# A hybrid decoder layer: how its first transfers, its warm-up and one row of scalings are laid out

## The chip, the cores and the metric

The kernel runs on one core of a Trainium2 chip. The time is device microseconds of the core, the median of several runs: 1089.81 us before, with runs from 1089.6 to 1090.01. The engines are TensorE (PE; its weight loads are shown as PEld), VectorE (DVE), ScalarE (ACT), GpSimd (POOL) and SyncE (SP). Transfers are issued on the queues of SP (q1 in the profile), ScalarE (q10) and GpSimd (q0).

## The reference, cut to what matters

One layer of 256 tokens by 2048 features, all in float32:

```python
h = rmsnorm(x, pre_norm_g)                  # x * rsqrt(mean(x*x) + eps) * g
proj = h @ w_in                             # 2048 x 18448, split into 11 parts
gk  = log_sigmoid(a_lr @ gla_gk_w2 + gla_gk_b) / 16      # forget gate
o_a = gated linear attention(a_q, a_k, a_v, gk)          # 4 heads
o_b = differential attention(b_q, b_k, b_v, lam)         # 16 heads
y_a = (rmsnorm(o_a) * silu(a_g)) @ w_branch_a
y_b = (rmsnorm(o_b) * 0.8 * silu(b_g)) @ w_branch_b
out = (sigmoid(m_a) * y_a + sigmoid(m_b) * y_b) @ w_out
return x + rmsnorm(out, post_norm_g)
```

The change touches the first steps: x, the gain `pre_norm_g`, and the first columns of `w_in`.

## The kernel before, in words

**Matmuls in three parts.** Every float32 product is made of three matmuls on rounded operands: high by high, high by low, low by high. So each weight tile that lands (`raw`) is split into `hi` (ScalarE, line 345) and `lo` (VectorE, line 346, which needs `hi`), and TensorE reads both. `hi` and `lo` have three buffers each. `take(key)` hands the next half tile to the matmuls and first traces the splits up to three half tiles ahead (`AHEAD = 3`); a split waits until TensorE is done with the buffer that it goes into.

**x.** x comes transposed, `xt[p, kt, t]` with 16 row tiles `kt`, in transfers that are interleaved with the first weights (`X_LOADS`). `prep_x(kt)` makes its high part `xs` on ScalarE (line 384: x times the gain `preg_s`) and the low part on VectorE (line 385). The row norm itself is applied later, as a factor of the results. For the first half tile the program writes an order out: `prep_x(0)`, then the high part of the first half of the weights' columns on VectorE (line 340), then that of the second on ScalarE (line 342).

**The beginning.** ScalarE's queue issues the gain (line 371). SP issues the first two row tiles of x (line 369), then the first two weight tiles, each in two halves, with x's next parts behind them (line 296 within `load`). VectorE fills `ones` and `ones_b` (lines 427, 429), and TensorE runs `WARM` matmuls on `ones_b` of `BRIDGE` columns (line 432), whose result nobody reads. Then `first_joint` takes the 16 row tiles of `v0` (832 columns each, in four banks; line 528), with `norm` in between (lines 454 on).

**Projections v2 and v3.** `token_major` (lines 554 to 562) takes eight half tiles of one group; each is twelve matmuls (line 551, or 540 through the helper `mm`). After each half tile of these two groups it calls `pump(2)`, which goes one step further in the first two of a list of tasks. The tasks are generators, in this order:

- `late`: the norm as a row, then lambda (three calls to its end)
- `forget_gate`: one call for the second stage's weights (lines 612 to 614), one for the low-rank part (617 to 625), two for the products and their bias (line 637, four instructions each on ScalarE), then absolute value (642) and exponential (644) of the first half, both of the second half, then logarithms (647)
- `sum_operands`: four calls that scale four row tiles of x each by the gain on ScalarE (line 686, in place), then sums of these on VectorE (lines 708 to 712), which are split in their turn as `s4`, `r1`, `s2` (lines 703, 704).

The sums are operands of the next phase, `block_products`, which replaces eight block products by seven.

**Who orders the work.** The program is traced in Python, and a scheduler of the framework then orders each engine's instructions: among those that are ready by its own estimate of time, the one traced earliest goes first. An instruction that is ready early can so be placed long before others that were traced ahead of it. `tc.keep_in_program_order(i)` ties `i` to come behind the instruction that was traced just before it on the same engine. `tc.issue_after` does the same behind a given instruction. Waits between engines are put in by the framework.

## Time and profile before

| | |
|---|---|
| median of 3 runs | 1089.81 us (1089.6 to 1090.01) |
| profiled execution, whole | 1092.18 us |
| its span in the profile | 1090.3 us |
| TensorE busy | 1082.4 us, 99% of the span |
| VectorE busy | 916.2 us, 84% |
| ScalarE busy | 711.2 us, 65% |
| moved by transfers | 285.06 MB, 261 GB/s over the span |

Rows of the timeline read: start in us, length in us, engine, line, operation, written tile, read tiles, shape, and how many instructions were merged into the row; in brackets the idle time of the engine before it and what ended that. "ACTq" and "SPq" are the issue of a transfer on that engine's queue. Rows of waits read: who waited for whom, us in total, how many times, the longest. Rows of a queue read: packets, MB, and the share of the sixteen engines' time.

### The profile page before, as it was taken

The page shows a single profiled execution, that of the slowest core. Times are in us where ns is not written, and L with a number is a line of the kernel's source. Part 1 is how long each engine was busy: PE and PEld are TensorE (multiplying, and loading weights), DVE is VectorE, ACT ScalarE, POOL GpSimd, SP SyncE. Part 2 cuts the span into 40 slices and gives each one's busy share as a digit, 9 for nine tenths or more (in the row PEclk, how much of TensorE's full clock was granted, in tenths as well). Part 3 has the DMA queues.
Part 4 walks back from the last instruction along what each step waited for, and adds up shares of the span by engine and source line. Part 5 has one row for each costly group of instructions (what it writes and reads, how often), then busy time and mean ns, then how long its engine had stood idle before and what let it go on. Part 6 is the DMA issues. An engine that isn't in the chain of part 4 may idle for free.

```text
span 1090.3 us, 15340 instructions
## 1 busy us (share of the span) xinstructions
PE 1082.4 (99%) x5451; PEld 929.4 (85%) x5451; DVE 916.2 (84%) x1277; ACT 711.2 (65%) x1038; POOL 146.4 (13%) x217
## 2 busy tenths in 40 slices
PE   9999999999999999999999999999999999999997
PEld 8999888888888888888888888889888888888886
DVE  7787987978979989889798999658779867889886
ACT  6986766666666766667665655556777765566662
POOL 0201111121021121211221100020111011100000
PEclk9999999999999999999999999999999999999999
DMA  9889969789798797997986654597988869979752
GB/s 338 286 288 325 265 232 319 182 274 298 248 331 223 277 303 192 337 258 261 300 228 228 255 177 171 176 333 253 284 279 271 277 238 315 350 255 270 270 183 107
DMA packets 63757, 285.06 MB, mean 261 GB/s; under 512 B 8320, under 2 KB 11392, under 8 KB 45504
## 3 DMA queue, kind: packets, MB, share of 16 engines
q1 hardware_dynamic: 39808, 186.87, 48.7%
q0 software_dynamic: 23296, 96.48, 32.6%
q8 instruction: 43, 0.70, 0.3%
q10 hardware_dynamic: 576, 0.73, 0.2%
q14 instruction: 34, 0.28, 0.1%
HBM read 258.88 MB, written 25.17 MB: 261 GB/s over the span
## 4 chain that ended last, share of the span: by engine, by line
PE 93%; DMA 3%; DVE 2%; issue 1%; ACT 1%; POOL 0%; POOLq 0%; SPq 0%; ACTq 0%; DVEq 0%
PE mm L540 57%; PE bg L540 26%; DMA raw<-in_w_dram 3%; PE mm L528 2%; PE bg L528 2%; PE mm L513 1%; DVE lo L346 1%; PE bg L956 1%; PE bg L513 1%; ACT hi L345 0%; PE bg L1121 0%; PE bg L1095 0%; PE bg L1096 0%; PE bg L1133 0%; PE bg L1134 0%
## 5 line engine op out<-in xcount | busy, mean ns | idle before, releaser
L345 ACT ACTIVATE hi<-raw 128x1024 fp32r<-128x1024 f32 (+3 forms) x261 | 268.4, 1032 | 209.1 <-PE bg L540 102.5
L346 DVE TENSOR_TENSOR lo<-raw,hi 128x1024 fp32r<-128x1024 f32 (+3 forms) x263 | 310.5, 1185 | 91.3 <-ACT hi L345 87.9
L540 PE MATMUL mm<-hi,xs 128*128 128x512 f32 (+1 forms) x848 | 214.1, 386 | 0.0
L540 PEld LDWEIGHTS mm<-hi,xs 128*128 128x128 f32 x848 | 156.9, 188 | 25.9
L540 PE MATMUL bg<-xs,hi 128*128 128x512 f32 x640 | 164.8, 389 | 0.0
L346 DVE TENSOR_TENSOR lo<-a,hi 128x1024 fp32r<-128x1024 f32 x112 | 135.0, 1219 | 11.7 <-ACT hi L345 10.5
L540 PEld LDWEIGHTS bg<-xs,hi 128*128 128x128 f32 x640 | 120.3, 188 | 23.4
L345 ACT ACTIVATE hi<-a 128x1024 fp32r<-128x1024 f32 x112 | 118.6, 1060 | 30.8 <-PE mm L540 22.8
L540 PE MATMUL mm<-lo,xs 128*128 128x512 f32 (+1 forms) x424 | 117.7, 383 | 0.0
L540 PEld LDWEIGHTS bg<-xs,lo 128*128 128x128 f32 x640 | 87.3, 190 | 6.2
L540 PEld LDWEIGHTS mm<-lo,xs 128*128 128x128 f32 x424 | 79.4, 188 | 14.5
L540 PE MATMUL bg<-xs,lo 128*128 128x256 f32 x640 | 89.2, 282 | 0.0
L346 DVE TENSOR_TENSOR lo<-b,hi 128x1024 fp32r<-128x1024 f32 x56 | 67.4, 1221 | 7.8 <-ACT hi L345 6.8
L345 ACT ACTIVATE hi<-b 128x1024 fp32r<-128x1024 f32 x56 | 59.3, 1061 | 18.1 <-PE mm L540 15.5
L540 PE MATMUL mm<-hi,oah 128*128 128x512 f32 x128 | 50.8, 397 | 0.0
L540 PE MATMUL mm<-hi,oal 128*128 128x512 f32 x128 | 50.0, 391 | 0.0
L1107 ACT ACTIVATE prob<-prob,mx,score_scale 128x128 f32<-128x128 f32 x64 | 34.2, 536 | 10.7 <-DVE mx L1102 10.6
L240 POOL DMA_DIRECT2D b<-in_w_dram x28 | 24.4, 873 | 107.3 <-DVE a L248 103.4
L540 PE MATMUL mm<-hi,obh 128*128 128x512 f32 x96 | 37.7, 392 | 0.0
L540 PE MATMUL mm<-hi,obl 128*128 128x512 f32 x96 | 37.4, 390 | 0.0
L345 ACT ACTIVATE hi<-c 128x1024 fp32r<-128x1024 f32 x28 | 29.6, 1060 | 10.2 <-PE mm L540 5.4
L248 DVE TENSOR_TENSOR a<-a,b 128x1024 f32<-128x1024 f32 x28 | 34.1, 1221 | 0.4
(409 smaller groups left out, 2021.1 us busy)
## 6 DMA issues: line engine op xcount, KB each, us to landing
raw<-in_w_dram SPq DMA_DIRECT2D x114, 1024.0 KB, 6.3
a<-in_w_dram POOLq DMA_DIRECT2D x28, 512.0 KB, 13.9
c<-in_w_dram SPq DMA_DIRECT2D x28, 512.0 KB, 8.7
b<-in_w_dram POOLq DMA_DIRECT2D x28, 512.0 KB, 7.9
a<-in_w_dram POOLq DMA_DIRECT2D x12, 1024.0 KB, 5.3
b<-in_w_dram POOLq DMA_DIRECT2D x12, 1024.0 KB, 8.8
raw<-in_w_dram SPq DMA_DIRECT2D x14, 832.0 KB, 6.5
dh<-dh POOLq DMA_DIRECT2D x16, 256.0 KB, 4.4
```

What stands on the lines that cost most here:

```text
L240: pool.dma_start(chain[s, name, i][:, c], weights(f"set{s}", 2 + i)[0][:, c], accum_op=ALU.add)
L248: dve.tensor_tensor(out=a, in0=a, in1=chain[s, "b", i][:, c] if second else raws[s, i, h], op=ALU.add)
L345: act.activation(hi_t[:, a:b], r[:, a:b], AF.Copy)
L346: dve.tensor_tensor(out=lo_t[:, a:b], in0=r[:, a:b], in1=f32(hi_t[:, a:b]), op=ALU.subtract)
L513: i = pe.matmul(out, lhs, rhs, start=first and n == 0, stop=last and n == len(pairs) - 1, **kw)
L528: i = pe.matmul(banks[g][b][:, :n], a[part][:, P * b : P * b + P], w[:, n * g : n * g + n], start=first, stop=last)
L540: i = pe.matmul(*args, **kw)
L956: pe.matmul(o, xk[:, P * c : P * c + P], xq.rearrange("p (b c t) -> p b c t", b=2, c=4)[:, :, c, :], start=i == 0, stop=i == 1)
L1107: act.activation(prob[m][:, lo:up], prob[m][:, lo:up], AF.Exp, scale=score_scale[:, b : b + 1], bias=mx[:, i : i + 1], accum_out=z[:, i : ...
```

## The change

- The host puts the 16 gains of each partition in front of x's rows. The tile `first_x` (16 + 2 x 256 floats a partition) takes the gains and the first two row tiles of x in one transfer on SP. `preg_s` becomes a view of it, and the transfer of its own on ScalarE's queue goes.
- The first half of the first weight tile is issued on ScalarE's queue, where the gains were; the second half and the rest stay on SP. `load(0)` is called right behind the transfer of `first_x` and ahead of ScalarE's table load.
- The readers of x's first two row tiles (`prep_x`, `square_x`, `sum_operands`) get them through `x_tiles`. `sum_operands` now writes to `xraw` what it read from `first_x` for these two, and in place for the others; each of its sixteen scalings is now kept in program order.
- The warm-up is 20 matmuls of 256 columns in place of 9 of 512, and its operand is filled ahead of `ones`.

```diff
-WARM = 9
+WARM = 20
-BRIDGE = 512
+BRIDGE = 256
...
         for a, b in zip(cuts, cuts[1:]):
-            i = sp.dma_start(raw[:, a:b], src[:, a:b])
+            i = (sp if j or a else act).dma_start(raw[:, a:b], src[:, a:b])
...
-    preg_s = const.tile([P, KT], F32, name="preg_s")
+    first_x = sm([P, KT + 2 * S], "first_x", bufs=1)
+    preg_s = first_x[:, :KT]
...
     def load_x(kt, n, queue=sp):
-        tc.keep_in_program_order(queue.dma_start(xraw[kt // 4][:, kt % 4 : kt % 4 + n, :], xt[:, kt : kt + n, :]))
-
-    tc.keep_in_program_order(act.dma_start(preg_s, preg))
-    load_x(0, 2)
+        src = xt[:, KT + S * kt : KT + S * (kt + n)].rearrange("p (a t) -> p a t", t=S)
+        tc.keep_in_program_order(queue.dma_start(xraw[kt // 4][:, kt % 4 : kt % 4 + n, :], src))
+
+    def x_tiles(kt, n):
+        if kt + n <= 2:
+            return first_x[:, KT + S * kt : KT + S * (kt + n)]
+        return xraw[kt // 4][:, kt % 4 : kt % 4 + n, :].rearrange("p a t -> p (a t)")
+
+    tc.keep_in_program_order(sp.dma_start(first_x, xt[:, : KT + 2 * S]))
+    load(0)
+    loaded[0] += 1
     act.preload_act_table_set("natural_log_exp_and_others")
...
     ones = const.tile([P, P], F32, name="ones")
-    dve.memset(ones, 1.0)
     ones_b = t2([P, BRIDGE], "ones_b").bitcast(BF16)[:, :BRIDGE]
     dve.memset(ones_b, 1.0)
+    dve.memset(ones, 1.0)
...
         for kt in range(KT):
             x = xraw[kt // 4][:, kt % 4, :]
-            act.activation(x, x, AF.Copy, scale=preg_s[:, kt : kt + 1])
+            tc.keep_in_program_order(act.activation(x, x_tiles(kt, 1), AF.Copy, scale=preg_s[:, kt : kt + 1]))
```

More of the change, by code (lines that the diff above doesn't have):

```diff
@@ L136, in hybrid_kernel @@
 @with_exitstack
-def hybrid_kernel(ctx: ExitStack, tc, xt, xn, preg, postg, w, w2, gkb, glag, lamv, diffg, ident_d, causal_d, lmask_d, out):
+def hybrid_kernel(ctx: ExitStack, tc, xt, xn, postg, w, w2, gkb, glag, lamv, diffg, ident_d, causal_d, lmask_d, out):
     nc = tc.nc
@@ L378, in prep_x @@
     def prep_x(kt):
-        i, j = kt // 4, kt % 4
-        src = xraw[i][:, j, :]
+        src = x_tiles(kt, 1)
         g = preg_s[:, kt : kt + 1]
@@ L392, in square_x @@
     def square_x(i):
-        src = xraw[i // 2][:, 2 * (i % 2) : 2 * (i % 2) + 2, :].rearrange("p a t -> p (a t)")
+        src = x_tiles(2 * i, 2)
         t = t2([P, 512], "xsq") if i else ssum
@@ L1611 @@
     arrays = {
-        "xt": np.ascontiguousarray(x.T.reshape(KT, P, S).transpose(1, 0, 2)),
+        "xt": np.concatenate([a["pre_norm_g"][0].reshape(KT, P).T, x.T.reshape(KT, P, S).transpose(1, 0, 2).reshape(P, -1)], axis=1),
         "xn": np.ascontiguousarray(x),
-        "preg": np.ascontiguousarray(a["pre_norm_g"][0].reshape(KT, P).T),
         "postg": np.ascontiguousarray(a["post_norm_g"][0]),
```

## The prediction

> **What bounds the kernel now.** I read the busy times first, then TensorE's waits, then the order of time around the change. The page has TensorE busy for nearly all of the span, and its own list of waits holds three:

> ```profile
> PE 1082.4 (99%) x5451; PEld 929.4 (85%) x5451; DVE 916.2 (84%) x1277; ACT 711.2 (65%) x1038; POOL 146.4 (13%) x217
> ```
> ```profile
> PE bg L432 <- DVE ones_b L429: 1.6, 1, 1.6
> PE bg L1571 <- ACT diag L1570: 1.0, 1, 1.0
> PE mm L528 <- ACT hi L342: 0.5, 1, 0.5
> ```

> The reader is to see that, apart from 1.0 us at the end, TensorE idles only before its first real matmul. So a microsecond won or lost at the start, and any new hole in its stream, reaches the end whole. There are then two questions: when and how fast do the first matmuls run, and does the change open a hole later? The start, in order of time:

> ```profile
> 0.74 0.41 ACTq L371 DMA_DIRECT2D preg_s<-in_preg_dram  x1
> 0.74 0.39 SPq L369 DMA_DIRECT2D xraw<-in_xt_dram  x1
> ...
> 0.83 0.17 DVE L427 MEMSET ones<- 128x128 f32 x1 [0.83 <-PEq L1626]
> 1.05 0.48 DVE L429 MEMSET ones_b<- 128x512 bf16 x1
> ...
> 1.18 0.89 SPq L296 DMA_DIRECT2D raw<-in_w_dram  x2
> ...
> 1.59 4.02 PE L432 MATMUL bg<-ones_b 128*128 128x512 bf16 x9 [1.59 <-DVE ones_b L429]
> ...
> 4.69 0.51 ACT L384 ACTIVATE xs<-xraw,preg_s 128x256 fp32r<-128x256 f32 x1 [2.23 <-DMA preg_s<-in_preg_dram]
> ...
> 5.23 0.49 DVE L385 SCALAR_TENSOR_TENSOR xs<-xraw,preg_s,xs 128x256 fp32r<-128x256 f32 x1 [3.69 <-ACT xs L384]
> 5.53 0.55 ACT L342 ACTIVATE hi<-raw 128x416 fp32r<-128x416 f32 x1 [0.34 <-DMA raw<-in_w_dram]
> 5.63 0.37 DVE L340 CAST hi<-raw 128x416 fp32r<-128x416 f32 x1
> ...
> 6.15 1.72 PE L528 MATMUL mm<-hi,xs 128*128 128x416 f32 x4 [0.54 <-ACT hi L342]
> ```

> Two chains meet at 6.15: x and the norm's weights (4.69, then 5.23 and 5.63 on VectorE) and the first weights (5.53 on ScalarE). VectorE ends at 6.00, ScalarE at 6.08. Neither alone can move the start by more than 0.08 us or so. The first matmuls also run slowly:

> ```profile
> 7.67 1.59 PE L528 MATMUL bg<-hi,xs 128*128 128x416 f32 x4
> 9.06 0.90 PE L528 MATMUL mm<-lo,xs 128*128 128x416 f32 x2
> 9.75 0.59 PE L528 MATMUL bg<-lo,xs 128*128 128x416 f32 x2
> ```

> Four starts from 7.67 to 9.06 are 0.35 us apart. Later, twelve matmuls of the same shape take 2.26 us (64.83 to 67.09 below), 0.188 each. So TensorE runs at about half rate until near 9.75, 3.6 us after the first real matmul. The nine warm-up matmuls (0.427 us apart, 3.84 us in all) did not bring it up.

> **The change, part by part.** *Warm-up.* The 256-column fill of ones comes first on VectorE, at 0.83 instead of 1.05, and at half of 0.48 or so. TensorE starts near 1.15. Twenty matmuls at half of 0.427 are 4.27 us and end at 5.42; nine were 3.84 and ended at 5.43. So the end stays, and the stretch is 0.43 us longer. That is worth nothing by itself, because the first real matmul waits for data. It counts only if it opens the full rate. The ten slow matmuls from 6.15 to 9.75 would take 1.88 us in place of 3.60, so the bounds are -1.7 and, if the opening comes a further 3.4 us late, +1.7. I take 0: the nearest row, 3.84 us of warm-up, shows no opening.

> [...]

> *Norm's weights in front of x, first weights on ScalarE's queue.* The small transfer goes. The first half tile of weights is issued at 0.74 on ScalarE, where the small one was, instead of 1.18 on SP; everything behind it on SP is issued some 0.4 earlier. But the two queues take turns. Here are their packets from 2.0 to 2.5 us:

> ```profile
> q1 hardware_dynamic: 50, 0.10, 92.9%
> q10 hardware_dynamic: 36, 0.00, 4.8%
> ```

> ScalarE's queue (q10) got 36 packets in while SP's (q1) got 50. Before, its packets were tiny; now each is a row of weights longer than a row of x, so x no longer lands well ahead of the weights. The earliest that x can be ready is near the 4.69 of before (start unchanged, or 0.3 sooner without the small transfer). The latest is with the weights as before, 5.53, which pushes the whole chain of 0.51, 0.49 and 0.37 back by 0.84. I take the middle, +0.4: first real matmul near 6.55. VectorE's order (x's low part, then the high part of the weights) makes the weights' earlier arrival useless.

> [...]

> *The sixteen ScalarE scalings of `sum_operands`.* This is a small line of the diff and, as I read it, the dear one. Unpinned, they ran in a slack stretch, long before they were needed:

> ```profile
> 33.35 2.50 ACT L686 ACTIVATE xraw<-xraw,preg_s 128x256 f32<-128x256 f32 x6
> ...
> 37.64 4.09 ACT L686 ACTIVATE xraw<-xraw,preg_s 128x256 f32<-128x256 f32 x10
> ```

> Each costs 0.41 us, 6.6 in all. Pinned, each goes behind the ScalarE instruction traced before it. `token_major("v2")` advances two tasks per half tile. `late` and `forget_gate` fill the first three steps, so the first four scalings are traced in the fourth, behind the last of `forget_gate`'s eight L637; the next four behind the first L642, then behind the first L644, then behind the second L642. That is the stretch in which ScalarE has no gap any more:

> ```profile
> 56.51 0.90 ACT L345 ACTIVATE hi<-raw 128x832 fp32r<-128x832 f32 x1 [1.37 <-PE mm L540]
> ...
> 57.93 1.06 ACT L703 ACTIVATE r1h<-temp 128x1024 fp32r<-128x1024 f32 x1
> 59.07 3.02 ACT L637 ACTIVATE gp<-bg,gkb_s 128x256 f32<-128x256 f32 x8
> 61.94 1.10 ACT L642 ACTIVATE e<-gp 128x1024 f32<-128x1024 f32 x1
> 62.89 0.94 ACT L345 ACTIVATE hi<-raw 128x832 fp32r<-128x832 f32 x1
> 63.67 1.10 ACT L644 ACTIVATE e<-e 128x1024 f32<-128x1024 f32 x1
> 64.63 0.94 ACT L345 ACTIVATE hi<-raw 128x832 fp32r<-128x832 f32 x1
> ...
> 66.36 0.94 ACT L345 ACTIVATE hi<-raw 128x832 fp32r<-128x832 f32 x1
> ...
> 68.10 0.79 ACT L664 ACTIVATE vh<-mm,rstd 128x208 fp32r<-128x208 f32 x2
> 68.73 0.95 ACT L345 ACTIVATE hi<-raw 128x832 fp32r<-128x832 f32 x1
> ```

> The reader is to see that this order is exactly the order of tracing (L642, split, L644, split, L642, split, L644, evacuation, split). So the four groups of 1.64 us will stand in it where they are traced, ahead of the splits. These splits (`hi`) are of v3's first four half tiles, and TensorE starts on those soon after:

> ```profile
> 64.83 1.49 PE L540 MATMUL mm<-hi,xs 128*128 128x416 f32 x7
> ...
> 67.09 1.11 PE L540 MATMUL mm<-hi,xs 128*128 128x416 f32 x5
> ...
> 69.36 0.92 PE L540 MATMUL mm<-hi,xs 128*128 128x416 f32 x4
> ...
> 71.62 0.55 PE L540 MATMUL mm<-hi,xs 128*128 128x416 f32 x2
> ```

> The slack is 64.83-63.83 = 1.0 for the first and 1.5 to 2.1 for the rest. Now the new chain, with 0.95 from each L642 or L644 to the next instruction, 0.78 from a split's start to the next start, 0.94 to its end, and 0.07 from there to TensorE (6.08 to 6.15 above). From 61.94: scalings to 63.58, L642 to 64.53, scalings to 66.17, first split ends 67.11, TensorE 67.18 in place of 64.83: +2.35. Then L644 from 66.95 to 67.91, scalings to 69.55, split ends 70.49, TensorE 70.56 where it was due 69.44: +1.1. L642 to 71.28, scalings to 72.92, split ends 73.86, TensorE 73.93 where due 72.83: +1.1. L644 to 74.65, evacuation (0.63) to 75.28, split ends 76.22, TensorE 76.29 where due 76.19: +0.1. Sum +4.65, call it 4.7. TensorE has no idle time later in which this could come back. Bounds: 0, if the scheduler sets the splits ahead; 6.6, if all of it counts. Between lies +3.0, if the eight L637 move up by some 1.7 into the place of `r1h` (57.93), which must now wait for the scalings, and the gap of 1.37 before 56.51.

> *What the scalings feed.* Sums and splits on VectorE wait for them:

> ```profile
> 61.48 1.29 DVE L712 SCALAR_TENSOR_TENSOR temp<-temp,xraw 128x512 f32<-128x512 f32 x2
> 62.68 1.22 DVE L704 TENSOR_TENSOR r1l<-temp,r1h 128x1024 fp32r<-128x1024 f32 x1
> ```

> They move back behind the last scalings, 72.92 in the chain above, among VectorE's `lo` splits. Bounds: 0, when they fit between these; +2.5, when these two stand ahead of one that is due. I take 0, because the new hole gives VectorE the same time.

> *The rest* (the function's argument, the view of x in the squares, the order of the two fills) moves no work of length. Cover for the later second fill: nothing reads `ones` before the norm, after the thirteenth row tile.

> *Sum.* 0 + 0.4 + 4.7 + 0 = +5.1. The profiled execution took 1092.18, a span of 1090.3 and 1.9 around it, so the changed one would take 1097.3 with a span near 1095.4. The median of the runs is 2.37 below the profiled time; it becomes 1089.81 + 5.1 = 1094.9.

> **The rivals.** *A: the scalings stay hidden.* The scheduler may set the splits ahead of them, or fill the idle stretch before 59.07 so that the chain begins earlier. For it: ScalarE has spare time before 56.51 (1.37) and `r1h`'s 1.06. Against it: the order above is the order of tracing. Time: only the start counts, +0.4, 1090.2 (1089.5 to 1091.9 with the start's bounds and a late full rate).

> *B: the warm-up opens the full rate before the first real matmul, and the scalings are hidden.* This ends below before. For it: the stretch is 0.43 longer than one that failed, and the rate did come 3.6 us into the next stretch. Against it: some 1.1 us without work lie between its end at 5.42 and 6.55. Its price is 1.7 less the 0.4 of x: -1.3, 1088.5; -2.0 with x early. It decides only if the rate has risen by 6.55 and the splits of v3 come no more than their slack of 1.0 late.

> *C: the full rate early, and the stall as forecast.* 4.7 - 1.3 = +3.4, 1093.2.

> **How the numbers follow.** Forecast 0.52, A 0.22, B 0.16, C 0.10. The forecast's own range is +2.7 to +7: 1092.5 to 1096.8. The whole range must take in A and most of B and leaves out the lower tail of B and the case of all bounds together: 1088.0 to 1096.6. About 0.2% (2.2 us) is what a measurement of this kernel can tell from no change. Slower by more: nearly all of the forecast and C, 0.60. Faster by more: B at its lower end and what I don't see in a schedule that is worked out anew, 0.10. Within: 0.30.

> **What would show it.** Right: the scalings of L686 stand between L637, L642 and L644 after 59 us, TensorE waits for a ScalarE split of v3 by some 2, 1 and 1 us, and `r1h` comes after 70. Wrong: L686 still before 45 us, or splits ahead of it and no new waits of TensorE. For the start: the first real matmul near 6.55, spaced 0.35 at first; 0.19 from the start would be B's step. A first matmul before 6.1 would show that x doesn't share its turns with the weights.

## The result and the profile after

The changed kernel takes 1098.93 us (median of six runs, 1098.75 to 1100.85), the kernel before, on the same chip, 1090.07 (six runs, 1089.6 to 1093.25). The ratio is 1.0083, with a 95% interval from 1.0068 to 1.0097: the change costs 8.9 us, where +5.1 was forecast. The direction was right, and most of the loss lies where it was forecast. The price was too low.

The profiled execution took 1100.72 us with a span of 1099.0; against 1092.18 and 1090.3 that is 8.5 more in the time and 8.7 in the span. All lines below the start of the kernel have moved by 7 (L637 is L644 now, L686 is L693, L540 is L547); the other changed numbers are named where they occur. First the busy times of the page:

```profile
PE 1085.0 (99%) x5462; PEld 931.5 (85%) x5462; DVE 914.8 (83%) x1277; ACT 711.6 (65%) x1038; POOL 147.1 (13%) x217
```

They say almost nothing: TensorE is busy for 2.6 us more, although it does eleven small matmuls more in the warm-up, and its share is still 99%. Its list of waits tells more (who waited for whom, us in total, times, the longest):

```profile
PE mm L547 <- ACT hi L345: 3.1, 2, 2.8
PE mm L535 <- ACT xs L391: 2.1, 1, 2.1
PE mm L547 <- DVE lo L346: 1.3, 3, 0.5
```

All three are new. One is at the start (`xs`), and two are for splits of weights behind it, the high ones of ScalarE and the low ones of VectorE. Here is ScalarE after in order of time, from the end of the low-rank part of the forget gate on:

```profile
60.54 3.03 ACT L644 ACTIVATE gp<-bg,gkb_s 128x256 f32<-128x256 f32 x8 [1.95 <-issue]
63.41 0.95 ACT L693 ACTIVATE xraw<-first_x 128x256 f32<-128x256 f32 x2
...
65.96 1.72 ACT L693 ACTIVATE xraw<-xraw,first_x 128x256 f32<-128x256 f32 x4
67.55 0.92 ACT L345 ACTIVATE hi<-raw 128x832 fp32r<-128x832 f32 x1
...
69.28 1.71 ACT L693 ACTIVATE xraw<-xraw,first_x 128x256 f32<-128x256 f32 x4
70.88 0.90 ACT L345 ACTIVATE hi<-raw 128x832 fp32r<-128x832 f32 x1
...
72.62 1.71 ACT L693 ACTIVATE xraw<-xraw,first_x 128x256 f32<-128x256 f32 x4
...
76.59 0.91 ACT L345 ACTIVATE hi<-raw 128x832 fp32r<-128x832 f32 x1
...
81.64 1.07 ACT L710 ACTIVATE r1h<-temp 128x1024 fp32r<-128x1024 f32 x1
```

The reader is to see that the four groups of scalings (L693) stand exactly where they are traced: the first two (63.41, whose second half is not shown, and 65.96) ahead of v3's first split (L345), the next two ahead of its second and third. No row between 60.54 and 86 has idle time in front of it, and `r1h` has gone from 57.93 to 81.64. TensorE's answer, in order of time; v3's first half tile is the row with 2.83 us of idle time, and the last row is the first matmul behind v3:

```profile
63.27 1.67 PE L547 MATMUL mm<-hi,xs 128*128 128x416 f32 x8
...
68.52 2.98 PE L547 MATMUL mm<-hi,xs 128*128 128x416 f32 x8 [2.83 <-ACT hi L345]
...
77.63 1.70 PE L547 MATMUL mm<-hi,xs 128*128 128x416 f32 x8
...
91.41 1.09 PE L547 MATMUL mm<-hi,xs 128*128 128x512 f32 x4
```

To place the loss, the same rows of before are needed: v2's last half tile and the first matmul behind v3 (v3's fourth half tile began at 71.62, a row that the prediction shows).

```profile
62.55 1.68 PE L540 MATMUL mm<-hi,xs 128*128 128x416 f32 x8
...
82.96 1.09 PE L540 MATMUL mm<-hi,xs 128*128 128x512 f32 x4
```

Up to v2's last half tile the delay is 63.27 - 62.55 = 0.72, all of it from the start. From there to v3's fourth half tile it takes 14.36 where it took 9.07: +5.29. From there to the first matmul behind v3 it takes 13.78 where it took 11.34: +2.44. The sum is 8.45; the two profiled executions differ by 8.5 in the time and by 8.7 in the span. So three stretches make the whole: the start, the one in which TensorE waits for ScalarE's splits, and the one behind v3's fourth half tile, in which the low splits of VectorE are waited for. For the third nothing had been put down. The stretches are not yet causes; the experiments part these. VectorE in the same time:

```profile
68.50 1.02 DVE L346 TENSOR_TENSOR lo<-raw,hi 128x832 fp32r<-128x832 f32 x1 [7.61 <-ACT hi L345]
71.03 0.69 DVE L715 TENSOR_TENSOR temp<-xraw,xraw 128x512 f32<-128x512 f32 x1 [1.51 <-ACT xraw L693]
...
80.80 1.22 DVE L711 TENSOR_TENSOR s4l<-temp,s4h 128x1024 fp32r<-128x1024 f32 x1
81.93 1.02 DVE L346 TENSOR_TENSOR lo<-raw,hi 128x832 fp32r<-128x832 f32 x1
```

VectorE stands still for 7.61 us in front of the late split. Before, sums stood in that place, 3.6 us of them (60.27 to 63.86, partly shown in the prediction); now they wait for the scalings. From 71 on all comes at once, and one of the low splits that TensorE waits for (81.93) stands behind `s4l`.

The start after, in order of time (x and the gains now land in `first_x`):

```profile
1.19 3.65 PE L439 MATMUL bg<-ones_b 128*128 128x256 bf16 x20 [1.19 <-DVE ones_b L435]
...
5.49 0.51 ACT L391 ACTIVATE xs<-first_x 128x256 fp32r<-128x256 f32 x1 [3.03 <-DMA first_x<-in_xt_dram]
...
6.95 1.43 PE L535 MATMUL mm<-hi,xs 128*128 128x416 f32 x4 [2.11 <-ACT xs L391]
```

x is there at 5.49 instead of 4.69, and the first real matmul behind it comes at 6.95 instead of 6.15. One profile of each could mislead, since the start differs between executions. Over all profiled executions of this document, ScalarE begins on x at 4.29 to 5.35 with the transfers of before (seven, six of them by 4.69) and at 5.11 to 5.53 with the weights on ScalarE's queue (four). The queues' packets between 3 and 4 us show why x is later:

```profile
q10 hardware_dynamic: 59, 0.20, 51.5%
q1 hardware_dynamic: 60, 0.13, 40.3%
```

In that microsecond the two queues move packets about one for one: 60 of x's queue (0.13 MB) and 59 larger ones of the weights (0.20 MB).

### The profile page after: what moved, and what is told of

Read it like the earlier page. It is cut to its first block, busy times and chain, and to the rows that moved or that the text cites. A ratio compares the mean times of both kernels' runs of the same rounds, so it can differ in the third digit from the quotient of the medians.

```text
span 1099.0 us, 15357 instructions
## 1 busy us (share of the span) xinstructions
PE 1085.0 (99%) x5462; PEld 931.5 (85%) x5462; DVE 914.8 (83%) x1277; ACT 711.6 (65%) x1038; POOL 147.1 (13%) x217
## 3 DMA queue, kind: packets, MB, share of 16 engines
q10 hardware_dynamic: 576, 1.15, 0.3%
## 4 chain that ended last, share of the span: by engine, by line
PE 95%; ACT 2%; issue 1%; DMA 0%; DVE 0%; POOL 0%; POOLq 0%; ACTq 0%
PE mm L547 58%; PE bg L547 27%; PE mm L535 2%; PE bg L535 2%; PE mm L520 1%; PE bg L963 1%; PE bg L520 1%; ACT xraw L693 1%; PE bg L1128 0%; ACT hi L345 0%; DMA first_x<-in_xt_dram 0%; PE bg L1102 0%; PE bg L1103 0%; PE bg L1141 0%; PE bg L1140 0%
## 5 line engine op out<-in xcount | busy, mean ns | idle before, releaser
L345 ACT ACTIVATE hi<-raw 128x1024 fp32r<-128x1024 f32 (+3 forms) x261 | 268.1, 1031 | 214.5 <-PE bg L547 100.8
L346 DVE TENSOR_TENSOR lo<-raw,hi 128x1024 fp32r<-128x1024 f32 (+3 forms) x263 | 309.5, 1181 | 93.6 <-ACT hi L345 87.4
L547 PE MATMUL mm<-hi,xs 128*128 128x512 f32 (+1 forms) x848 | 215.6, 388 | 3.2 <-ACT hi L345 3.1
L547 PEld LDWEIGHTS mm<-hi,xs 128*128 128x128 f32 x848 | 157.4, 189 | 30.3 <-ACT hi L345 4.2
L547 PE MATMUL bg<-xs,hi 128*128 128x512 f32 x640 | 164.8, 389 | 0.0
L346 DVE TENSOR_TENSOR lo<-a,hi 128x1024 fp32r<-128x1024 f32 x112 | 134.8, 1218 | 11.2 <-ACT hi L345 10.0
L547 PEld LDWEIGHTS bg<-xs,hi 128*128 128x128 f32 x640 | 120.3, 188 | 23.4
L345 ACT ACTIVATE hi<-a 128x1024 fp32r<-128x1024 f32 x112 | 118.6, 1060 | 29.8 <-PE mm L547 21.9
L547 PE MATMUL mm<-lo,xs 128*128 128x512 f32 (+1 forms) x424 | 118.6, 385 | 1.3 <-DVE lo L346 1.3
L547 PEld LDWEIGHTS mm<-lo,xs 128*128 128x128 f32 x424 | 79.7, 189 | 17.0 <-DVE lo L346 2.5
L547 PEld LDWEIGHTS bg<-xs,lo 128*128 128x128 f32 x640 | 87.3, 190 | 6.2
L547 PE MATMUL bg<-xs,lo 128*128 128x256 f32 x640 | 89.2, 282 | 0.0
L346 DVE TENSOR_TENSOR lo<-b,hi 128x1024 fp32r<-128x1024 f32 x56 | 67.4, 1220 | 7.9 <-ACT hi L345 6.8
L345 ACT ACTIVATE hi<-b 128x1024 fp32r<-128x1024 f32 x56 | 59.3, 1060 | 18.2 <-PE mm L547 15.8
L547 PE MATMUL mm<-hi,oah 128*128 128x512 f32 x128 | 50.8, 397 | 0.0
L547 PE MATMUL mm<-hi,oal 128*128 128x512 f32 x128 | 50.0, 391 | 0.0
L547 PE MATMUL mm<-hi,obh 128*128 128x512 f32 x96 | 37.7, 392 | 0.0
L547 PE MATMUL mm<-hi,obl 128*128 128x512 f32 x96 | 37.4, 390 | 0.0
L345 ACT ACTIVATE hi<-c 128x1024 fp32r<-128x1024 f32 x28 | 29.6, 1060 | 10.5 <-PE mm L547 5.7
```

Of the source, the lines that this page charges most:

```text
L345: act.activation(hi_t[:, a:b], r[:, a:b], AF.Copy)
L346: dve.tensor_tensor(out=lo_t[:, a:b], in0=r[:, a:b], in1=f32(hi_t[:, a:b]), op=ALU.subtract)
L547: i = pe.matmul(*args, **kw)
```

## The experiments

The theory at the outset: the pin (the call that keeps the sixteen scalings in program order) makes nearly all of the loss. It makes ScalarE's chain late, TensorE then runs at half rate behind the hole (below), which was taken to cost some 1.7 us, and VectorE's sums come late in their turn; the start makes about 1 us, and the warm-up nothing. The rivals: the loss comes from the start and its clock; ScalarE's load alone makes it, and the low splits are late only because the high ones are; the halved rate costs nothing.

### The pin alone, twice

```diff
-            act.activation(x, x, AF.Copy, scale=preg_s[:, kt : kt + 1])
+            tc.keep_in_program_order(act.activation(x, x, AF.Copy, scale=preg_s[:, kt : kt + 1]))
```

> The kernel before, with the sixteen scalings kept in program order and nothing else. Theory 1 (the order of the scalings makes nearly all of the loss: the direct waits for ScalarE's splits, 3.6 us, TensorE's rate halved for 3.4 us behind the long wait, 1.7, and VectorE's late lo splits, 2.4): 7 to 8 us slower than before, some 1097.5 to 1098, and waits of TensorE for hi and lo between 60 and 90 us. Rival (the sum on record is right for the scalings, the rest comes from the transfers and the warm-up): 4 to 5 us slower, 1094.5.

Measured: 1097.52 us against 1090.26, ratio 1.0069 (1.0055 to 1.0083), +7.3. The same kernel went again beside the run with the filled hole, further down:

> pin_alone once more, on the same chip and in the same rounds as filled_hole: 1097.5, with v3's first half tile at half rate.

There its ratio was 1.0075 (1.0062 to 1.0088), some +8.2 on 1090.01. Its profile, TensorE from v2's last half tile on:

```profile
60.77 1.67 PE L540 MATMUL mm<-hi,xs 128*128 128x416 f32 x8
...
66.01 2.00 PE L540 MATMUL mm<-hi,xs 128*128 128x416 f32 x8 [2.83 <-ACT hi L345]
...
75.12 1.71 PE L540 MATMUL mm<-hi,xs 128*128 128x416 f32 x8
...
88.89 1.09 PE L540 MATMUL mm<-hi,xs 128*128 128x512 f32 x4
```

From v2's last half tile to v3's fourth: 14.35; on to the end of v3: 13.77. These are the two later stretches of the changed kernel to 0.01 us, and together 5.28 + 2.43 = 7.7. So the pin, and nothing else in the diff, makes both.

### The change without the pin, and with half of it

```diff
-            tc.keep_in_program_order(act.activation(x, x_tiles(kt, 1), AF.Copy, scale=preg_s[:, kt : kt + 1]))
+            act.activation(x, x_tiles(kt, 1), AF.Copy, scale=preg_s[:, kt : kt + 1])
```

> The changed kernel without the order on the sixteen scalings: they go back to 33 to 42 us, the first two of them to the very beginning behind x. Theory 1: only the start's loss stays, +0.4 to +1.2 us (1090.5 to 1091.3), and TensorE has no wait after its first real matmul. Rival (transfers and warm-up carry half of the loss): +4 us.

Measured: 1091.25 against 1090.26, ratio 1.0009 (1.0000 to 1.0018), +1.0. Fourteen scalings are back in the slack stretch, and TensorE waits for no split of v3. The scalings of the first two row tiles, which no longer overwrite what they read, stand at 5.52 and 7.65 us, the first of them ahead of a split that the first real matmul waits for. Of the fourteen, the last six:

```profile
36.36 2.50 ACT L693 ACTIVATE xraw<-xraw,first_x 128x256 f32<-128x256 f32 x6
```

This fits the theory. +1.0 without the pin and +7.3 to +8.2 with the pin alone add up to 8.3 to 9.2, around the 8.9 of the whole.

In the next kernel only row tiles 8 to 15 are pinned, so that the last two of the four groups stay:

```diff
-            tc.keep_in_program_order(act.activation(x, x_tiles(kt, 1), AF.Copy, scale=preg_s[:, kt : kt + 1]))
+            (tc.keep_in_program_order if kt >= 8 else (lambda i: i))(act.activation(x, x_tiles(kt, 1), AF.Copy, scale=preg_s[:, kt : kt + 1]))
```

> The changed kernel with the last eight of the sixteen scalings kept in order and the first eight free. By the chain of the prediction the first split of v3 then comes in time, the second 0.2 us late, the third 1.1, the fourth 0.1: 1.4 us in short waits. Theory 1 (the halved rate comes from one long wait, the lo waits from the late sums): no halved rate after 60 us, 1.4 for ScalarE and up to 2.4 for VectorE, start +1: 3.5 to 5 us slower than before. Rival (what counts is the number of scalings, each alike): half of the 7.3 us that the order costs alone, and the start, +4.6, with the rate halved as well.

Measured: 1096.16 against 1090.27, ratio 1.0056 (1.0044 to 1.0069), +5.9: half of the scalings cost two thirds of the whole, more than either the theory (3.5 to 5) or its rival (4.6) had. TensorE from v2's last half tile on:

```profile
61.76 1.68 PE L547 MATMUL mm<-hi,xs 128*128 128x416 f32 x8
...
72.96 1.68 PE L547 MATMUL mm<-hi,xs 128*128 128x416 f32 x8
...
86.72 1.09 PE L547 MATMUL mm<-hi,xs 128*128 128x512 f32 x4
```

11.20 to v3's fourth half tile (+2.13 on before's 9.07) and 13.76 from there (+2.42). The first of these stretches costs less than half, for the slack of v3's first splits takes its part. The second costs the whole: each sum reads row tiles of the second half, directly or through another sum, so relative to v3's fourth half tile the first one is as late with eight late scalings as with sixteen (6.6 us ahead of it in both). But what ScalarE still has to do from there on is the same in both as well, so this run does not yet part VectorE from ScalarE.

### ScalarE's load without late sums

The kernel before, with sixteen extra scalings of the same size into a tile that nobody reads, pinned at the same places; the kernel's own scalings stay free.

```diff
+        spare = sm([P, 4, S], "spare", bufs=1)
         for kt in range(KT):
+            if kt % 4 == 0:
+                for j in range(kt, kt + 4):
+                    tc.keep_in_program_order(act.activation(spare[:, j % 4, :], xs[0][:, 0, 0, :].bitcast(F32), AF.Copy, scale=preg_s[:, j : j + 1]))
```

> The kernel before, whose own sixteen scalings stay early, with sixteen more of the same size, written to a tile that nobody reads, kept in program order in the places where the change puts its own. ScalarE carries the same load there, and VectorE's sums aren't late. Theory 1: the ScalarE waits and the halved rate without VectorE's part, 4.5 to 5.5 us slower (1095), and no TensorE wait for lo of note. Rival (the waits for lo come from ScalarE's lateness alone): 7 to 8 us slower, with the waits for lo.

Measured: 1095.94 against 1090.26, ratio 1.0051 (1.0038 to 1.0063), +5.7. In TensorE's list of waits one row is for a split:

```profile
PE mm L540 <- ACT hi L345: 3.2, 3, 2.1
```

The waits for high splits are there, three of them, and those for low splits (L346) are gone. The sums are early in this kernel, so the low splits' lateness comes from them and not from ScalarE's. The +5.7 is a little above the theory's 4.5 to 5.5, and TensorE's rows say where it lies (v2's last half tile begins at 60.60):

```profile
74.18 1.79 PE L540 MATMUL mm<-hi,xs 128*128 128x416 f32 x8
...
77.51 1.77 PE L540 MATMUL mm<-hi,xs 128*128 128x416 f32 x8 [0.79 <-ACT hi L345]
...
86.84 1.09 PE L540 MATMUL mm<-hi,xs 128*128 128x512 f32 x4
```

To v3's fourth half tile it takes 13.58 (+4.51), and from there 12.66 (+1.32), without any late sum. The third wait for a high split is that of v3's fifth half tile: it begins 3.33 us after the fourth, where 2.27 is usual. So ScalarE's load alone makes over half of the loss behind the fourth half tile. In the changed kernel the fifth comes 3.24 after the fourth (80.87 - 77.63), so the first of its waits for a low split delays nothing that ScalarE would not have delayed. What late sums add to ScalarE's load is the difference to the pinned kernel of the same rounds: 1097.52 - 1095.94 = 1.6.

### Late sums without ScalarE's load

The reverse: the scalings stay free, and the six additions on VectorE that make `r1`, `s2` and `s4` are kept in program order.

```diff
-            dve.tensor_tensor(out=rows(r1, q), in0=part(1, 1, q), in1=part(1, 0, q), op=ALU.subtract)
+            tc.keep_in_program_order(dve.tensor_tensor(out=rows(r1, q), in0=part(1, 1, q), in1=part(1, 0, q), op=ALU.subtract))
...
-            dve.scalar_tensor_tensor(out=rows(s4, q), in0=rows(s2, q), scalar=-1.0, in1=part(0, 1, q), op0=ALU.mult, op1=ALU.subtract)
+            tc.keep_in_program_order(dve.scalar_tensor_tensor(out=rows(s4, q), in0=rows(s2, q), scalar=-1.0, in1=part(0, 1, q), op0=ALU.mult, op1=ALU.subtract))
```

(and so for `s2`, between these two)

> The kernel before with one edit: the six additions of VectorE that form the sums r1, s2 and s4 (L708, L709, L712) are kept in program order, so that they stand behind v3's fourth low split as in the changed kernel, while ScalarE's scalings stay at 33 to 42 us and its splits on time. Theory V (VectorE's late sums are a cost of their own, 2.4 us of the loss): no wait for a high split of v3, but waits of TensorE for low splits of v3 between 70 and 85 us, and +1.5 to +2.5, that is 1091.8 to 1092.8 against some 1090.2. Rival (the low splits are late only because ScalarE's chain has made everything late together): no such wait and within 0.5 of before.

Measured: 1094.7 against 1090.4, ratio 1.0040 (1.0028 to 1.0053), +4.3. TensorE waits for no high split, and for two low ones:

```profile
PE mm L540 <- DVE lo L346: 2.2, 2, 1.8
```

The second of the two and what follows, in order of time:

```profile
78.66 1.02 PE L540 MATMUL mm<-lo,xs 128*128 128x416 f32 x4 [1.81 <-DVE lo L346]
...
81.87 1.75 PE L540 MATMUL mm<-lo,xs 128*128 128x416 f32 x4
83.42 1.75 PE L540 MATMUL mm<-hi,xs 128*128 128x416 f32 x8
```

The theory's side, but beyond its 1.5 to 2.5: late sums alone cost 4.3, where they add 1.6 to a late ScalarE. There TensorE itself is late by then, 5.3 us in the changed kernel, which leaves VectorE time for some of them; here it is on time and meets all of them. So 5.7 for ScalarE's load and 4.3 for the sums, each alone, do not add up to the 7.3 to 8.2 of both.

### Is the halved rate part of the price?

Behind the hole of 2.83 us, v3's first eight matmuls took 2.98 us where eight take 1.67. The granted clock in the changed kernel, in stretches of 1 us (start and end, length, TensorE's busy time and number of matmuls, its clock, share of the transfers, GB/s):

```profile
7.00:8.00 1.00, 1.00 (x4) 0.64 1.02 399
...
10.00:11.00 1.00, 1.00 (x5) 0.65 1.02 430
68.00:69.00 1.00, 0.48 (x2) 0.86 0.00 0
...
72.00:73.00 1.00, 1.00 (x6) 0.93 0.00 0
```

To test whether this is part of the loss, the pinned kernel got six matmuls of float32 that nobody reads into the hole:

```diff
-            half_tile(banks, n, q, ops, *take(key))
+            pair = take(key)
+            if key == "v3" and q == 0:
+                spare = ps("bg")
+                for kt in (1, 3, 4, 5, 6, 7):
+                    i = pe.matmul(spare[:, :S], ident, xraw[kt // 4][:, kt % 4, :], start=True, stop=True)
+                    tc.keep_in_program_order(i)
+            half_tile(banks, n, q, ops, *pair)
```

> pin_alone with six matmuls that nobody reads ahead of v3's first real one on TensorE; each reads a row tile that one of the first eight scalings has just written, so that they lie within the long wait. They make no data come sooner. Theory (the rate is halved because TensorE stands nearly idle for 2.8 us): v3's first half tile runs at full rate, its twelve matmuls in 2.3 us in place of 3.9, and the whole is 1 to 1.7 us faster than pin_alone, 1095.8 to 1096.5. Rival (the slow half tile is slow for another reason, such as the engines' load on the memory): as pin_alone, 1097.5, or slower.

Measured: 1098.10 against 1090.01, ratio 1.0071 (1.0059 to 1.0083), +8.1, beside +8.2 of the pinned kernel in the same rounds. The filling kept the full rate, for eight matmuls take 1.78 now, and nothing came of it:

```profile
63.01 3.02 PE L561 MATMUL bg<-xraw,ident 128*128 128x256 f32 x12
66.00 1.78 PE L540 MATMUL mm<-hi,xs 128*128 128x416 f32 x8
...
69.33 1.78 PE L540 MATMUL mm<-hi,xs 128*128 128x416 f32 x8 [0.79 <-ACT hi L345]
```

v3's second half tile begins at 69.33 in both, as all later ones do to 0.01 us. What TensorE gains by its rate, it spends waiting for the next high split. So this part of the theory fell: the halved rate fills time in which TensorE would have waited anyway.

In the kernel with late sums it isn't free. There nothing holds v3's last half tile but the four low matmuls ahead of it, which take 1.55 (81.87 to 83.42) where 0.76 is usual, so some 0.8 of its 4.3 us is the rate.

### The warm-up alone

The kernel before with the changed warm-up:

```diff
-WARM = 9
+WARM = 20
-BRIDGE = 512
+BRIDGE = 256
...
-    dve.memset(ones, 1.0)
     ones_b = t2([P, BRIDGE], "ones_b").bitcast(BF16)[:, :BRIDGE]
     dve.memset(ones_b, 1.0)
+    dve.memset(ones, 1.0)
```

> The kernel before with the warm-up of 20 matmuls of 256 columns and its operand filled first, transfers as before. If 4.27 us of warm-up reach the full rate and the gap of some 1.3 us to 6.15 is too short to lose it: 1.7 us faster in a profile where before was slow to 9.75, 0 to -1.7 in the medians. Rival (the rate is lost again in the gap, as in the changed kernel): 0, with first matmuls 0.35 us apart.

Measured: 1090.20 against 1090.26, ratio 1.0001 (0.9992 to 1.0009). By itself, the new warm-up is worth nothing that these runs can tell, either way.

### The first weights on SP's queue again

The changed kernel with one edit:

```diff
-            i = (sp if j or a else act).dma_start(raw[:, a:b], src[:, a:b])
+            i = sp.dma_start(raw[:, a:b], src[:, a:b])
```

> The changed kernel with one edit: the first half tile of weights goes on SP's queue behind first_x again. Theory Q (sharing turns between the two queues is the whole cost of the new start): x is there near 3.6 instead of 5.5 us, the start costs nothing or less, and the rest of the loss stays: +7 to +8, 1097.2 to 1098.2. Rival (the start's cost comes from the shorter cover of the warm-up or the larger first transfer): the first real matmul stays behind 6.6 us and the time stays at +8.9, near 1099.

Measured: 1098.03 against 1090.4, ratio 1.0069 (1.0055 to 1.0083), +7.6 in place of +8.9. x is there early:

```profile
3.48 0.51 ACT L391 ACTIVATE xs<-first_x 128x256 fp32r<-128x256 f32 x1 [1.47 <-DMA first_x<-in_xt_dram]
```

So the weights on a second queue are what delays x, by 2.0 us (5.49 against 3.48) against the same transfer with both in one queue; and in one queue the start costs nothing that shows beside the pin's 7.3 to 8.2, as theory Q has it.

### In search of a version that wins

Three kernels without late scalings. The first takes the change, but traces the scalings of row tiles 0 and 1 beside the last row tiles of v0, and leaves the others free:

```diff
+            if j in (14, 15):
+                tc.keep_in_program_order(act.activation(xraw[0][:, j - 14, :], x_tiles(j - 14, 1), AF.Copy, scale=preg_s[:, j - 14 : j - 13]))
...
-            tc.keep_in_program_order(act.activation(x, x_tiles(kt, 1), AF.Copy, scale=preg_s[:, kt : kt + 1]))
+            if kt >= 2:
+                act.activation(x, x_tiles(kt, 1), AF.Copy, scale=preg_s[:, kt : kt + 1])
```

> The changed kernel with the scalings of x's first two row tiles traced beside its last two (kept in order there, near 33 us) and the other fourteen free: all sixteen lie in the slack stretch as before, none at the very beginning. Theory: only the start's loss, x waiting for its turns beside the weights of the other queue: +0.4 to +0.9 us. Rival (the merged transfer and the longer warm-up pay): 0 or faster.

The second is the first with the weights on SP's queue:

```diff
-            i = (sp if j or a else act).dma_start(raw[:, a:b], src[:, a:b])
+            i = sp.dma_start(raw[:, a:b], src[:, a:b])
```

> As early_scale, but the first half tile of weights stays on SP behind x: gains merged with x, warm-up of the change. Theory (the turns between two queues cost the start): first real matmul at 6.0 to 6.1, 0.4 to 0.8 us ahead of early_scale, and -0.3 to +0.1 us against before. Rival (the queue makes no difference): as early_scale.

The third is the second with a longer warm-up, to leave TensorE no gap in front of the first real matmul:

```diff
-WARM = 20
+WARM = 30
```

> As weights_on_sp with 30 warm-up matmuls in place of 20. If the rate rises within the warm-up, ten more cost 1.1 us at full rate and end near the first real matmul; the rate is then lost in fewer executions: median -0.3 to 0 against before and fewer runs 1.5 us or more above the fastest. If it rises late, the warm-up ends behind 7 us and the start is late by about 1.

Measured, against 1090.27: 1091.63 (ratio 1.0013, 1.0005 to 1.0022), 1090.21 (0.9997, 0.9988 to 1.0006), and 1091.04 (1.0006, 0.9997 to 1.0015). The first is slower than its theory's 0.4 to 0.9. The step from the first to the second, -1.4, is the price of ScalarE's queue once more. The second has x at 3.56, some 1.1 earlier than before, and its first real matmuls at 5.29, earlier than the 6.0 expected, yet it is no faster than before. Its third row tile begins at 10.61, and in the second profile of the pinned kernel, which has the transfers of before, at 10.63: what the early x gained is gone by then. ScalarE stands still for 1.83 us ahead of 7.46 until weights land, so the weights' transfers are the likely limit, which no run tests. The third was expected at -0.3 to 0 and lies 0.8 above the second; its first real matmul comes at 6.40, behind the longer warm-up. No version beats the kernel before.

## Where the prediction was right, and which steps failed

**The bound.** It said that a new hole in TensorE's stream reaches the end whole. It did, nearly: 8.45 us at the end of v3, 8.1 at TensorE's last matmuls (1092.65 against 1084.57) and 8.5 in the whole time.

**The order of the scalings.** Right in every position: scalings behind the eight L637, then L642, scalings, split, L644, scalings, split, as forecast, and `r1h` behind 70. From the end of the eight L637 to the end of v3's fourth split the forecast had 76.22 - 61.94 = 14.28; it took 77.50 - 63.41 = 14.09.

**The steps that failed** both concern what lies behind v3's fourth half tile. The prediction put nothing there, and 2.44 us came.

*VectorE's sums, put at 0.* It had the bound right (+2.5) and took the wrong end, "because the new hole gives VectorE the same time". The hole gave the time, but VectorE could not use it: all the work that could have filled the hole waited for the same scalings that made it. Its 7.61 us of idle time stand in the very place. The kernel with the extra scalings has early sums and no wait for a low split; the kernel with late sums alone has such waits. On top of ScalarE's load they add 1.6 us.

*ScalarE's chain, put at 4.7 and ended too soon.* The chain was followed to v3's fourth half tile, where only +0.1 was left, and ended there. One more step of it would have shown more: from the fourth split to the fifth ScalarE needed 3.31 before (68.73 to 72.04), while TensorE needs 2.27 for a half tile, so the fifth comes about 1.0 late. The kernel with the extra scalings shows this: 4.51 to the fourth half tile, near the forecast's 4.7, then 1.32 more, and +5.7 in all.

**Why the stretch to the fourth half tile took 5.29 in the changed kernel, and not 4.5 to 4.7.** The error is not in that part of the chain but in its beginning. The prediction left the eight L637 at their place, with a bound that let them move up by 1.7. They came later: 63.41 - 61.94 = 1.47, of which 0.72 is the start. ScalarE's 1.95 of idle time in front of them says why. They wait for TensorE's products L641, which stand behind four low matmuls now:

```profile
59.27 0.91 PE L547 MATMUL mm<-lo,xs 128*128 128x416 f32 x4
60.02 1.14 PE L641 MATMUL bg<-lrt,w_s 128*128 128x256 f32 x8
```

Before, they stood ahead of them:

```profile
58.58 1.11 PE L634 MATMUL bg<-lrt,w_s 128*128 128x256 f32 x8
59.53 0.93 PE L540 MATMUL mm<-lo,xs 128*128 128x416 f32 x4
```

So the scheduler's order changed on another engine too, at a place that the diff doesn't touch. This goes with the late sums and not with ScalarE's load. The products stand behind the low matmuls in the kernel with late sums alone too (57.49 behind 56.74), and in all others whose sums are late; in the kernel with the extra scalings they stand ahead of them, as before (56.63 ahead of 57.59). So of the 5.29 the later beginning, 0.75, belongs to the sums as well.

**The term of the transfers, +0.4, was +0.7** in the profile (0.8 at the first real matmul), inside its bounds and near the upper one: x came at 5.49, where the latest forecast was 5.53. In the medians the new start costs 1.0 to 1.4, beyond that bound. The +0.4 was the middle between two bounds; 59 packets of the weights against 60 of x's queue between 3 and 4 us go with the upper one.

**The term of the warm-up, 0, was right, and its reason wrong.** Its upper bound, +1.7, let the full rate come a further 3.4 us late, a length that no row of before shows. No run shows such a delay: in the changed kernel it came 3.75 us behind the first real matmul (10.70 - 6.95), where before has 3.6. The prediction read from one profile that nine warm-up matmuls don't bring the rate up. In the second profile of the pinned kernel, with those nine, they did:

```profile
6.03 0.99 PE L528 MATMUL mm<-hi,xs 128*128 128x416 f32 x4 [0.41 <-DVE hi L340]
```

Four matmuls in 0.99, not 1.72. In its first profile they did not (four in 1.73 at 6.82), and those two executions of one kernel took 1100.48 (the first) and 1097.75. Of these 2.7, 0.8 is the later first matmul. The profiled execution of before was one of the late ones. At v2's last half tile it is 1.8 behind the second profile of the pinned kernel (62.55 against 60.77), which accounts for most of the 2.4 by which it stood above its median.

**The rivals.** A (scalings hidden) is what the kernel without the pin does: 1091.25, within A's 1089.5 to 1091.9, if not at its 1090.2. B's step came halfway in the profiled execution: the rate did rise within the new warm-up (20 matmuls in 3.65, not 4.27), but that ended the warm-up sooner, at 4.84, and left TensorE 2.11 us of idle time, behind which the rate was lost again, from 7.28 to 10.70. C needs the same step and fell with it.

**The sum.** By stretches it is 0.72 + 5.29 + 2.44 = 8.45 in place of 5.1. By causes, in the medians, it is 5.7 for ScalarE's load (forecast 4.7), 1.6 for the sums (0) and 1.0 to 1.4 for the start (0.4), in all 8.3 to 8.7 beside the measured 8.9. The range ended at +6.8 because it left out the case that several terms lie near their upper bounds.

**Open.** What the start costs in the median is known only from differences between kernels (+1.0 without the pin, two scalings at the start included; 1.3 and 1.4 for the queue). Why late sums make the scheduler put the products behind the low matmuls was not looked into. What decides whether a warm-up of one length opens the rate in an execution was not settled.

## What to carry to other kernels

An instruction that is pinned to its place in the program takes that place's price, not its own: sixteen scalings that were free at 33 us cost 7 to 8 us at 63, with all that waits for them, on an engine that is busy for 65% of the span, since in that stretch it has no gap. When work moves back, follow the chain until the engine has its slack again, not only until one delay is small. Follow also what reads the result, and don't credit the readers with the hole that the move makes, because they wait for the same thing. And of two transfers that were needed at once here, the one needed first came 2.0 us earlier at the head of one queue than when the other went beside it on a second queue.

## What the runs showed of the hardware that was not expected

**The full rate was lost behind idle times of 1.81 to 2.83 us, but not behind each.** In the changed kernel it was lost after 2.11 us without work in one case and 2.83 in the other, and in the kernel with late sums after 1.81:

```profile
80.00:81.00 1.00, 1.00 (x5) 0.59 1.03 425
```

That places the loss at 80.18, 1.5 us behind the end of the idle time (78.66); in the changed kernel it came 0.33 and 0.20 behind (7.28 - 6.95, 68.72 - 68.52). The length does not decide alone. In the changed kernel with the weights on SP's queue the same hole of 2.83 us cost no rate, for eight matmuls behind it took 1.81, and the granted clock from 60 to 92 us was 1.00:

```profile
67.47 1.81 PE L547 MATMUL mm<-hi,xs 128*128 128x416 f32 x8 [2.83 <-ACT hi L345]
```

What decides beside the length was not shown.

**The granted clock was silent on the first slow matmuls.** In the first profile of the pinned kernel, four matmuls from 8.34 take 1.59 us, where four from 11.81 take 0.92, and the row of that stretch has a clock of 1.00:

```profile
8.00:10.00 2.00, 2.00 (x7) 1.00 1.05 428
```

So at the start of this kernel the rate has to be read from the matmuls' own spacing.
